# Reordering a two-layer encoder on one core: gates and neighbourhood attention first, retention after them, branch a's product ahead of branch b's block

## The chip, the core and the metric

The kernel runs on one core of a Trainium2 chip. A core has five engines that work side by side, each through its own instruction stream: TensorE (PE: matmuls), VectorE (DVE), ScalarE (ACT), GpSimd (POOL) and SyncE (SP, which here only starts DMA transfers). They share an on-chip memory of 128 partitions (SBUF) and an accumulator memory that TensorE writes (PSUM). The metric is the device time of one execution in microseconds; the median over runs is compared.

## What is computed

A bidirectional encoder of two layers over 512 tokens of width 1024. Cut to what matters:

```python
for i in range(2):
    q_na,k_na,v_na, q_r,k_r,v_r,g_r, gate_a,gate_b = split(x @ w_in[i])
    ya = neighbourhood_attention(q_na, k_na, v_na, rpb[i])        # 8 heads of 64, softmax
    yb = silu(g_r) * groupnorm(retention(q_r, k_r, v_r))          # 4 heads, both directions
    merged = sigmoid(gate_a)*(ya @ w_a[i]) + sigmoid(gate_b)*(yb @ w_b[i])
    x = layer_norm(alpha*x + merged @ w_out[i])                   # token sublayer
    ffn = (gelu(a) * b) @ w_down[i]      # a, b: halves of conv3(x @ w_up[i])
    x = layer_norm(alpha*x + ffn + sigmoid(x @ w_pg[i]) * (p[i] @ w_pp[i]))
```

## The kernel before

Every product is made in about fp32 precision from two halves: a number is split into hi (rounded) and lo (the rest), and each product is three matmuls, hi·hi, lo·hi and hi·lo (`mm3`, L395). A weight chunk is 128x1024 (512 KB). It arrives by DMA as raw, ScalarE makes hi, and VectorE makes lo = raw - hi (`split`, L164). For the chunks in SENT it goes another way: ScalarE makes hi and -hi, and a DMA on POOL's queue that adds while it writes makes lo from the copy of the weights in HBM (L355 to L357).

The four 1024-wide parts of the input projection that are largest (v, g of the retention branch, and the two gates) and branch b's projection are each a block of seven half-size products in place of eight, with sums of weights and sums of activations as operands. The seven are called a, c, t1, d, t2, t3, t4. Blocks 0 and 1 are v and g, blocks 2 and 3 the gates; "3t1" is product t1 of block 3. The weights of t1 to t4 are sums of chunks. `add` (L298) makes such a sum in one of two ways: by a DMA on POOL's queue that adds the second chunk from HBM (L305), or, for the products named in ON_CHIP, by a tensor_tensor of POOL on a chunk that is in SBUF already (rawa or rawt + rawd, L302). The activation sums s are made by VectorE from the transposed x (xf).

A layer's token sublayer has these steps. `vg` walks the table VG: blocks in an order written out by hand, with a few head projections between. Then come the "fillers" in the order of FILL: q and k heads of retention with their rotary step, q and k of neighbourhood attention (nq, nk), and its v (vn). After each filler a slot ends, and the tables RET_AT and NA_AT say in which slot each step of a retention head or of a neighbourhood head is issued. The last seven fillers are branch b's block (`bb`, L1085), whose `emit` multiplies each finished quarter into M, the gate of branch b. In one of its slots `plain_x` loads the residual xn; in layer 1 it also multiplies by the norm's scale and adds its shift, on POOL (L1080, L1081). After the fillers branch a's product follows, and `merge` (L1203) multiplies it with gate a into sa and adds M (L1205, L1206). `turn` (L1208) transposes the merged tile and splits it into mt; `proj_ln` makes the output projection and the layer norm. In a neighbourhood head the exponentials S are scaled by the reciprocal of their sums, rc, by one POOL instruction over 128x1024 (L1035), before TensorE transposes them.

Two things set the order of instructions. From the start, and in the MLP, each engine's instructions are kept in the order of the code; these show line 96 in the profile whatever their own line. From the end of `vg` to the end of the token sublayer a scheduler orders them by their dependencies and shows their own lines. In both, each engine takes its own instructions strictly in turn. Weights are fetched and split ahead of use in the order of one list, `Stream.seq`, with three raw buffers (rp), three pairs of hi and lo buffers (wp), and a pool of thirty 4 KB units (up) for all else.

Of the kernel before, what the change touches and what calls it, by code (L numbers as in the profile page):

```python
# [32 lines left out]
SENT = ((24, 36),)  # L33
# [4 lines left out]
FILL = (('nq0', 'q1', 'nk0', 'k2', 'k1', 'vn', 'q2', 'q3', 'k3', 'nq1', 'nk1', 'nq2', 'nq3', 'nk3', 'nk2'),  # L38
 ('k1', 'q1', 'nk0', 'nk2', 'nq0', 'nq1', 'q2', 'q3', 'k2', 'k3', 'vn', 'nk1', 'nq2', 'nk3', 'nq3'))
BB = ("a", "c", "t1", "d", "t2", "t3", "t4")  # L40
RET_AT = ((5, 6, 13, 14), (3, 5, 11, 11))
NA_AT = ((6, 11, 14, 16, 18, 19, 19, 19), (10, 13, 16, 16, 16, 19, 19, 19))
ORD = ('vector', 'scalar', 'tensor', 'gpsimd', 'sync')
RESIDENT = {(l, c) for l in range(DEPTH) for c in range(68, 72)}
# [3 lines left out]
VG = (('p0', 'p1', '2a', '3a', '3c', '2c', '2t1', '2t2', '3t1', '2d', '3t2', '2t3', '3d', '1a', '3t3', '3t4', '2t4', '0a', '0c', '1c', '0t1', '0d', 'q0',  # L48
  '0t2', '1t1', '0t3', '0t4', 'k0', '1d', '1t2', '1t3', '1t4'),
 ('2a', '2c', '3a', '3c', '3t1', '2t1', '3t2', '2d', '3d', '2t2', '0a', '2t3', '3t3', '0c', '2t4', '1a', 'q0', '0t1', '3t4', '0d', '0t2', '1c', '1t1',  # L50
  '1d', '0t3', '0t4', '1t2', 'k0', '1t3', '1t4'))

XN_AT = 5
M_AT = 4
TABLES_AT = (12, 15)
REST_AT = (1, 3, 5, 8, 10, 12)
PEND_AT = (2, 3)
# [12 lines left out]
VG_HELD = (('0c', '0t1', '1t1', '1t2', '1t4', '2c', '2d', '2t2', '2t3', '3a', '3d', '3t2', '3t3', '3t4'),  # L70
 ('0t1', '0t2', '0t3', '0t4', '1t2', '1t4', '2a', '2c', '2d', '2t1', '2t2', '2t4', '3c', '3t1', '3t2', '3t3'))
ON_CHIP = ('t3', 't2 t3', 't2 t3', 't2 t3')
BB_HELD = ('a', 't1', 't2')
BB_EARLY = 'c'
# [38 lines left out]
def trunk(tc, wpack, x_nat, x_tr, head, p_tr, rpb, decay, ln_par, ln_col, conv, cos_t, sin_t, dist, xi_d, zd, ident_d, out):  # L113
# [4 lines left out]
    with ExitStack() as es:  # L118
# [49 lines left out]
        class Item:  # L168
# [7 lines left out]
            def __init__(self, kind, src, width, pool=None, plus=None, own=None):  # L176
# [4 lines left out]
                self.sent = kind == "w" and any(a <= src[1] < b for a, b in SENT)  # L181
# [40 lines left out]
        def vg_items(l):  # L222

            by = {}
            for b, c0 in enumerate((0, 12, 52, 36)):
                pos = {(q, j): (l, c0 + 2 * i + j, 0, 1024) for i, q in enumerate("acbd") for j in range(2)}
                for it in block_items(pos, {k[1:]: up for k in VG_HELD[l] if k[0] == str(b)}, VG_EARLY, ON_CHIP[b]):
                    it.block = b
                    by.setdefault(f"{b}{it.kind}", []).append(it)
            return [it for k in VG[l] for it in (by[k] if k in by else plain_items(l, k))]  # L230

        def bb_items(l):
# [3 lines left out]
            for it in block_items(pos, {k: up for k in BB_HELD}, BB_EARLY):  # L236
                by.setdefault(it.kind, []).append(it)
# [409 lines left out]
        for l in range(DEPTH):  # L647
# [574 lines left out]
            for t in range(4):  # L1222
                turn(1, t)
# [492 lines left out]
```

## Time and profile before

| | |
|---|---|
| median of 3 runs | 1759.23 us (1758.42 to 1760.92) |
| profiled execution | 1758.02 us, of it span 1756.3 us |
| TensorE busy | 1683.0 us, 96% of the span |
| VectorE busy | 1316.5 us, 75% |
| ScalarE busy | 945.4 us, 54% |
| POOL busy | 294.7 us, 17% |
| mean granted clock of TensorE | 0.982 |
| moved by DMA | 277.35 MB |

Busy time of an engine is the time in which it runs instructions; a wait is idle time before an instruction, shown with the instruction that released it. A group row reads: line, engine, operation, output<-inputs, shapes, count | busy us, mean ns of one | idle time before and what ended it. "PE u L96 <- ACT s L96: 9.8, 1, 9.8" says that TensorE waited 9.8 us in one wait, before a matmul into u, for ScalarE's s. PEclk is the clock granted to TensorE, in tenths in the page's slices (9 is 90% or more) and as a fraction in the stretch table. The token sublayers lie at about 0 to 440 us and 880 to 1320 us, the MLPs behind each.

### The profile page before, as it was taken

The numbers are of one execution on the slowest core, as the hardware profiler recorded it, in microseconds if no ns is written. First come the engines' busy times: TensorE is split into PE (matmuls) and PEld (weight loads), VectorE is DVE, ScalarE is ACT, GpSimd is POOL, SyncE is SP. The second block draws the span as 40 slices with busy tenths as digits, with TensorE's granted clock in tenths as the row PEclk, the third lists the DMA queues.
The fourth block names the chain that finished last, engine by engine and source line by source line (L and its number), as shares of the span: only waits on it lengthen the run. The fifth ranks groups of instructions, "written<-read, shape, count | busy, mean of one in ns | idle before, by whom it ended". The sixth has DMA issues, their size and how long they took to land.

```text
span 1756.3 us, 21209 instructions
## 1 busy us (share of the span) xinstructions
PE 1683.0 (96%) x7815; PEld 1395.4 (79%) x7815; DVE 1316.5 (75%) x1908; ACT 945.4 (54%) x1434; POOL 294.7 (17%) x238
## 2 busy tenths in 40 slices
PE   9699999999999999999988999998889999999997
PEld 7587888877888888888876778887668888888886
DVE  5867568898687867667877766867986878676678
ACT  6555576773266545345555655568622665443452
POOL 1504011320110100000142220122421101000003
PEclk9899999999999999999999999999989999999999
DMA  8686455764754535527766745367538546356375
GB/s 284 186 250 171 108 138 127 173 176 152 219 144 133 131 113 164 143 85 204 199 219 175 200 119 132 85 156 187 161 117 255 144 129 136 107 160 141 96 203 96
DMA packets 81896, 277.35 MB, mean 158 GB/s; under 512 B 9473, under 2 KB 9985, under 8 KB 81793
## 3 DMA queue, kind: packets, MB, share of 16 engines
q1 hardware_dynamic: 60768, 201.55, 33.3%
q0 software_dynamic: 21024, 74.46, 24.8%
q8 instruction: 61, 1.00, 0.2%
q14 instruction: 43, 0.34, 0.1%
HBM read 257.10 MB, written 17.83 MB: 157 GB/s over the span
## 4 chain that ended last, share of the span: by engine, by line
PE 79%; DVE 11%; ACT 4%; DMA 3%; issue 2%; SPq 0%; POOL 0%; DVEq 0%; ACTq 0%; POOLq 0%
PE gt L96 28%; PE u L96 15%; PE v L96 7%; PE w L96 4%; PE gn L398 3%; PE gn L399 3%; PE gn L397 3%; PE gt L399 2%; PE gt L397 2%; PE gt L398 2%; DVE lo L166 2%; DVE lo L96 2%; PE x L96 2%; DVE s L96 1%; ACT hi L96 1%
## 5 line engine op out<-in xcount | busy, mean ns | idle before, releaser
L96 PE MATMUL gt<-x1t,hi 128*128 128x512 f32 x1408 | 433.4, 389 | 0.0
L96 PEld LDWEIGHTS gt<-x1t,hi 128*128 128x128 f32 x1408 | 264.3, 188 | 54.7
L96 PE MATMUL gt<-x1t,lo 128*128 128x512 f32 x704 | 274.1, 389 | 0.1
L96 DVE TENSOR_TENSOR lo<-raw,hi 128x1024 fp32r<-128x1024 f32 (+1 forms) x146 | 174.8, 1206 | 48.5 <-ACT hi L96 48.2
L96 DVE TENSOR_TENSOR lo<-rawa,hi 128x1024 fp32r<-128x1024 f32 x122 | 148.4, 1228 | 72.3 <-ACT hi L96 71.9
L96 DVE SCALAR_TENSOR_TENSOR ca<-gt,cw,ca 128x511 f32<-128x511 f32 x176 | 131.8, 749 | 79.1 <-ACT ca L96 76.0
L96 ACT CAST hi<-raw 128x1024 fp32r<-128x1024 f32 (+1 forms) x149 | 153.0, 1037 | 37.8 <-PE u L96 13.5
L96 PEld LDWEIGHTS gt<-x1t,lo 128*128 128x128 f32 x704 | 132.1, 188 | 28.5 <-DVE lo L96 1.0
L96 ACT CAST hi<-rawa 128x1024 fp32r<-128x1024 f32 x122 | 122.9, 1021 | 52.1 <-DMA rawa<-in_wpack 17.5
L96 ACT ACTIVATE ca<-gt,cw 128x512 f32<-128x512 f32 x88 | 68.6, 779 | 131.4 <-PE gt L96 131.4
L96 POOL DMA_DIRECT2D rawa<-in_wpack x80 | 70.0, 900 | 390.8 <-DVE lo L96 336.6
L96 PE MATMUL u<-hi,s 128*128 128x512 f32 x320 | 105.0, 401 | 11.0 <-ACT s L96 9.8
L96 PE MATMUL v<-hi,s 128*128 128x512 f32 x320 | 106.3, 404 | 9.5 <-ACT hi L96 7.7
L399 PE MATMUL gt<-xt,lo 128*128 128x512 f32 x224 | 87.5, 391 | 1.5 <-DMA lo<-in_wpack 0.8
L397 PE MATMUL gt<-xt,hi 128*128 128x512 f32 x224 | 87.9, 393 | 0.0
L398 PE MATMUL gt<-xt,hi 128*128 128x512 f32 x224 | 87.3, 390 | 0.0
L96 PE MATMUL u<-hi,xt 128*128 128x512 f32 x256 | 81.1, 390 | 3.1 <-DVE p L96 3.1
L96 PEld LDWEIGHTS v<-hi,s 128*128 128x128 f32 x320 | 63.0, 197 | 24.8 <-ACT hi L96 9.0
L96 PEld LDWEIGHTS u<-hi,s 128*128 128x128 f32 x320 | 62.2, 195 | 25.1 <-ACT s L96 10.2
L165 ACT CAST hi<-raw 128x1024 fp32r<-128x1024 f32 x41 | 43.1, 1051 | 57.4 <-PE gn L399 26.0
L96 PE MATMUL v<-lo,s 128*128 128x512 f32 x160 | 65.3, 408 | 6.4 <-DVE lo L96 6.4
L166 DVE TENSOR_TENSOR lo<-raw,hi 128x1024 fp32r<-128x1024 f32 x41 | 50.7, 1237 | 26.6 <-ACT hi L165 26.3
(366 smaller groups left out, 3932.3 us busy)
## 6 DMA issues: line engine op xcount, KB each, us to landing
raw<-in_wpack SPq DMA_DIRECT2D x207, 512.0 KB, 4.1
rawa<-in_wpack POOLq DMA_DIRECT2D x90, 512.0 KB, 5.9
rawa<-in_wpack SPq DMA_DIRECT2D x34, 512.0 KB, 6.4
rawt<-in_wpack SPq DMA_DIRECT2D x34, 512.0 KB, 7.1
lo<-in_wpack POOLq DMA_DIRECT2D x24, 512.0 KB, 5.9
rawt<-in_wpack POOLq DMA_DIRECT2D x18, 512.0 KB, 6.6
rawd<-in_wpack SPq DMA_DIRECT2D x16, 512.0 KB, 9.6
r_scr<-pp SPq DMA_DIRECT2D x8, 512.0 KB, 12.1
```

The lines of the kernel that those rows point to most:

```text
L96: r = f(*a, **k)
L165: nc.scalar.copy(hi, src)
L166: nc.vector.tensor_sub(lo, src, _f(hi))
L397: nc.tensor.matmul(ps, lh, rh, start=start, stop=False, skip_group_check=more)
L398: nc.tensor.matmul(ps, lh, rl, start=False, stop=False, skip_group_check=more)
L399: nc.tensor.matmul(ps, ll, rh, start=False, stop=stop, skip_group_check=more)
```

## The change

The token sublayer is put in another order. VG is now short: it starts with the gate blocks 3 and 2 and a few projections of neighbourhood attention. All else moves to FILL: the rest of the gate blocks, vn and the other na projections, then blocks 0 and 1 (v and g) with the q and k heads, then "ba", branch a's product, and at the end branch b's block. Neighbourhood heads stand early in the slots and retention heads late. `fillers` can therefore emit block products, and only the short VG is kept in the order of the code; the rest is ordered by the scheduler.

With it come: the softmax scaling in four 128x256 pieces, on ScalarE for the heads in RC_ACT (6 and 3 of 8), on VectorE for the others; layer 1's xn operations on VectorE; ON_CHIP empty but for t2 of block 2 in layer 0, so that the other sums of weights are made by accumulating DMA; SENT by names of items, 7 chunks in place of 24; `ba`, which multiplies branch a's product by its gate into sa before branch b's block; the sum with M inside that block's `emit` (L1146, L1147 of the new kernel); turns inside the block, one product late (TURN_LAG); the first half of the output projection made token by token, with its four chunks resident; and new slots for smaller steps.

In counts of instructions: matmuls and transposes 7,828 as before, VectorE 1,910 to 1,963, ScalarE 1,372 to 1,402, of which table loads 30 to 41, POOL 243 to 202, transfers started by SP 424 as before. POOL's tensor_tensor sums of weights fall from 28 to 2, its scalings from 16 to 0, its xn operations from 8 to 0, while its transfers rise by 9, and lo<-hi on ScalarE falls from 24 to 7.

```diff
-FILL = (('nq0', 'q1', 'nk0', 'k2', 'k1', 'vn', 'q2', 'q3', 'k3', ...
+FILL = (('2c', '3t2', '3d', 'nk1', 'vn', '3t3', '3t4', '2t1', 'nk2', '2t2', '2d', '2t3', '0a', 'nq2', ...
-RET_AT = ((5, 6, 13, 14), (3, 5, 11, 11))
+RET_AT = ((33, 32, 38, 37), (31, 38, 36, 39))
-SENT = ((24, 36),)
+SENT = (('k3', 'q2'), ('k2', 'k3', 'nk2', 'nq3', 'q1'))
-VG = (('p0', 'p1', '2a', '3a', '3c', '2c', '2t1', '2t2', '3t1', ...
+VG = (('p0', 'p1', '3a', 'nq0', 'nk3', 'nq3', '3c', '3t1', 'nk0', '2a', 'nq1'), ('3a', '2a', '2c', '3c', '3t1', ...
-ON_CHIP = ('t3', 't2 t3', 't2 t3', 't2 t3')
+ON_CHIP = (('', '', 't2', ''), ('', '', '', ''))
+RC_ACT = ((0, 2, 3, 5, 6, 7), (3, 4, 6))
...
-                s4 = S.rearrange("p (g n) -> p g n", g=4)
-                nc.gpsimd.tensor_tensor(s4, s4, _ap(rc, 0, [[1, 4], [0, 256]]), ALU.mult)
+                for g in range(4):
+                    if h in RC_ACT[l]:
+                        nc.scalar.activation(S[:, g * 256:(g + 1) * 256], S[:, g * 256:(g + 1) * 256], AF.Copy, scale=rc[:, g:g + 1])
+                    else:
+                        nc.vector.tensor_scalar_mul(S[:, g * 256:(g + 1) * 256], S[:, g * 256:(g + 1) * 256], rc[:, g:g + 1])
...
                     if l:
-                        nc.gpsimd.tensor_tensor(z, z, g, ALU.mult)
-                        nc.gpsimd.tensor_tensor(z, z, b, ALU.add)
+                        nc.vector.tensor_mul(z, z, g)
+                        nc.vector.tensor_add(z, z, b)
...
+            def ba():
+                for t in range(4):
+                    sa.append(unit_f("sa"))
+                    nc.sync.dma_start(sa[t], gscr[0][t * P:(t + 1) * P, :])
+                for hb in range(2):
+                    pss = []
+                    for t in gemm_n_tok(lambda k, s, t: yat[k][:, s, t * P:(t + 1) * P], 2, pss, 0):
+                        c = slice(hb * 512, (hb + 1) * 512)
+                        nc.vector.tensor_mul(sa[t][:, c], pss[t], sa[t][:, c])
+                        if t % 2:
+                            yield
...
                     nc.vector.scalar_tensor_tensor(m, src, sign, m, op0=ALU.mult, op1=ALU.mult)
+                    nc.vector.tensor_add(sa[t][:, c], sa[t][:, c], m)
+                    turns.append((hb, t))
...
+                    due = len(turns)
                     step(kind)
+                    for _ in range(due if TURN_LAG else len(turns)):
+                        turn(*turns.pop(0))
                     yield
+                for z in turns:
+                    turn(*z)
...
-            def merge(hb, t, ps):
-                c = slice(hb * 512, (hb + 1) * 512)
-                nc.vector.tensor_mul(sa[t][:, c], ps, sa[t][:, c])
-                nc.vector.tensor_add(sa[t][:, c], sa[t][:, c], M[t][:, c])
```

What this does to the instruction streams is shown at three places. The first is POOL in layer 0's first blocks. Before, with rawa and rawt the chunks that become a sum, and rawd the chunk that is added:

```order
L96 DMA rawa_158<-in_wpack 128x1024
L96 TENSOR_TENSOR rawa_117<-rawa_117,rawd_358 128x1024
L96 TENSOR_TENSOR rawa_121<-rawa_121,rawd_401 128x1024
L96 DMA rawa_117<-in_wpack 128x1024
L96 DMA rawa_121<-in_wpack 128x1024
L96 TENSOR_TENSOR rawt_84_458<-rawt_84_458,rawd_358 128x1024
L96 TENSOR_TENSOR rawa_123<-rawa_123,rawd_477 128x1024
L96 TENSOR_TENSOR rawt_88_480<-rawt_88_480,rawd_401 128x1024
L96 TENSOR_TENSOR rawa_158<-rawa_158,rawd_519 128x1024
```

and now:

```order
L98 DMA rawa_117<-in_wpack 128x1024
L98 DMA rawa_121<-in_wpack 128x1024
L98 DMA rawa_411<-in_wpack 128x1024
L98 DMA rawa_463<-in_wpack 128x1024
L98 DMA rawt_115_652<-in_wpack 128x1024
L98 DMA rawa_117<-in_wpack 128x1024
L98 DMA rawt_121_679<-in_wpack 128x1024
L310 DMA rawa_121<-in_wpack 128x1024
L307 TENSOR_TENSOR rawa_411<-rawa_411,rawd_1069 128x1024
L307 TENSOR_TENSOR rawa_463<-rawa_463,rawd_1088 128x1024
```

The tensor_tensor sums between the transfers are gone but for two, and transfers that add from in_wpack stand in their place.

The second is ScalarE in layer 0's start, around the first block product. Before (hi: a weight half; p: the copy of a product; s and xt: halves of activations):

```order
L96 CAST hi_264<-raw_208 128x1024
L96 COPY p_47_282<-u_244 128x512
L96 COPY p_48_283<-u_245 128x512
L96 CAST hi_296<-raw_210 128x1024
L96 CAST hi_312<-raw_250 128x1024
L96 COPY p_56_328<-u_294 128x512
L96 COPY p_57_329<-u_295 128x512
L96 CAST hi_338<-raw_268 128x1024
L96 CAST hi_354<-rawa_117 128x1024
L96 ACT_TABLE_LOAD
L96 ACTIVATE p_56_328<-p_56_328 128x512
L96 ACTIVATE p_57_329<-p_57_329 128x512
```

and now, where gate block 3 is first, and the next matmuls are those of nq0 on all of xt:

```order
L98 CAST hi_245<-raw_123 128x1024
L98 CAST hi_263<-raw_158 128x1024
L98 COPY p_44_281<-u_243 128x512
L98 COPY p_45_282<-u_244 128x512
L98 CAST xt_106<-xf_125 128x2x256
L98 CAST xt_106<-xf_127 128x2x256
L98 CAST xt_106<-xf_125 128x2x256
L98 CAST xt_106<-xf_127 128x2x256
L98 ACTIVATE dl_299<-dl_299 128x16
L98 CAST hi_320<-raw_204 128x1024
```

The casts of the second half of x (xf_125, xf_127) now stand directly behind the copies of the first product, and ahead of all further weights.

The third is VectorE at layer 1's last turns, with M branch b's gated product, sa the merged tile, mt its transposed halves. Before, where xn stands on POOL (rows not shown):

```order
L1109 SCALAR_TENSOR_TENSOR M_10571<-u_10226,M_10571 128x512
L1109 SCALAR_TENSOR_TENSOR M_10573<-u_10227,M_10573 128x512
L166 TENSOR_TENSOR lo_10845<-raw_10665,hi_10844 128x1024
L1205 TENSOR_TENSOR sa_10776<-gn_10784,sa_10776 128x512
L1206 TENSOR_TENSOR sa_10776<-sa_10776,M_10222 128x512
L1205 TENSOR_TENSOR sa_10778<-gn_10799,sa_10778 128x512
L1206 TENSOR_TENSOR sa_10778<-sa_10778,M_10224 128x512
L1205 TENSOR_TENSOR sa_10780<-gn_10814,sa_10780 128x512
L1206 TENSOR_TENSOR sa_10780<-sa_10780,M_10571 128x512
```

and now:

```order
L1146 SCALAR_TENSOR_TENSOR M_10879<-u_10575,M_10879 128x512
L1146 SCALAR_TENSOR_TENSOR M_10881<-u_10576,M_10881 128x512
L1147 TENSOR_TENSOR sa_10243<-sa_10243,M_10879 128x512
L1147 TENSOR_TENSOR sa_10245<-sa_10245,M_10881 128x512
L1094 TENSOR_TENSOR xn_10939<-xn_10939,lng_10935 128x1024
L1095 TENSOR_TENSOR xn_10939<-xn_10939,lnb_10936 128x1024
L1094 TENSOR_TENSOR xn_10943<-xn_10943,lng_10935 128x1024
L1094 TENSOR_TENSOR xn_10947<-xn_10947,lng_10935 128x1024
L1095 TENSOR_TENSOR xn_10943<-xn_10943,lnb_10936 128x1024
L1095 TENSOR_TENSOR xn_10947<-xn_10947,lnb_10936 128x1024
L1094 TENSOR_TENSOR xn_10951<-xn_10951,lng_10935 128x1024
L168 TENSOR_TENSOR mt_10995<-tr_10989,mt_10994 128x4x128
```

Branch a's product (gn) no longer stands between the additions to sa; the eight xn operations came from POOL, and the halves mt of the last turns stand behind them.

More of the change, by code (lines that the diff above doesn't have):

```diff
@@ L485, in proj_ln @@
             deep = 4 + follow
-            drain(gemm_n(lh, nchunk, [], post=lambda t, ps: half(t, 0, ps), ahead=lambda c: max(2, deep - 2 * (nchunk + n1 - 1 - c))))
+            pss = []
+            for t in gemm_n_tok(lh, nchunk, pss, 0):
+                half(t, 0, pss[t])
             pss = []
```

108 lines of the change are left out of this document (57 added, 51 removed), and 3 rows, old and new, of the table FILL.

## The prediction

> **What bounds the kernel now.** I read the page's engine shares first, then the clock and POOL slices.
>
> ```profile
> PE 1683.0 (96%) x7815; PEld 1395.4 (79%) x7815; DVE 1316.5 (75%) x1908; ACT 945.4 (54%) x1434; POOL 294.7 (17%) x238
> POOL 1504011320110100000142220122421101000003
> PEclk9899999999999999999999999999989999999999
> ```
>
> TensorE is the bound, and the change leaves its 7,828 matmuls as they are. So only time in which TensorE waits, or runs at a lower granted clock, can move. The stretch table says where that is (columns: stretch, length, busy time of PE, PEld, DVE, ACT, POOL, then granted clock, DMA share, GB/s).
>
> ```profile
> 44.00:110.00 66.00, 50.72 (x200) 40.22 (x201) 51.12 (x64) 39.40 (x52) 26.30 (x14) 0.87 0.69 189
> 110.00:176.00 66.00, 62.54 (x275) 51.02 (x274) 45.80 (x42) 37.16 (x49) 22.37 (x12) 1.00 0.74 215
> 360.00:400.00 40.00, 37.80 (x185) 30.97 (x186) 38.63 (x75) 27.45 (x59) 8.38 (x6) 0.96 0.63 165
> 400.00:440.00 40.00, 37.41 (x186) 30.81 (x185) 32.19 (x46) 15.44 (x24) 0.00 (x0) 1.00 0.47 150
> 440.00:880.00 440.00, 439.95 (x1965) 364.45 (x1964) 331.75 (x447) 218.82 (x299) 40.25 (x43) 1.00 0.56 153
> 880.00:920.00 40.00, 35.25 (x155) 28.35 (x154) 30.54 (x29) 23.29 (x36) 15.76 (x8) 0.96 0.67 223
> 920.00:960.00 40.00, 34.61 (x138) 27.36 (x137) 30.93 (x24) 20.81 (x28) 13.66 (x10) 0.91 0.72 173
> 960.00:1040.00 80.00, 75.00 (x321) 60.78 (x320) 53.88 (x51) 44.66 (x57) 22.20 (x13) 0.98 0.61 177
> 1220.00:1260.00 40.00, 38.84 (x208) 33.13 (x208) 37.74 (x75) 30.10 (x64) 8.28 (x6) 0.97 0.63 172
> 1260.00:1290.00 30.00, 17.91 (x65) 13.79 (x64) 29.88 (x25) 8.64 (x14) 22.69 (x8) 0.79 0.21 79
> ```
>
> From 440 to 880 (layer 0's MLP) 1965 matmuls fill the time at full clock: 440 / 1965 = 0.224 us each. With that as the yardstick, a stretch's length minus 0.224 times its matmuls is what it loses, waits and low clock together: 66 - 44.8 = 21.2 us in 44–110, 4.4 in 110–176, 5.3 in 880–920, 9.1 in 920–960, 8.1 in 960–1040, 15.4 in 1260–1290. These six make 63.5 us, and they are the stretches in which POOL is busy. The waits of TensorE name VectorE and ScalarE as the late ones:
>
> ```profile
> PE u L96 <- ACT s L96: 9.8, 1, 9.8
> PE u L397 <- DVE p L708: 8.5, 1, 8.5
> PE v L96 <- DVE lo L96: 6.4, 5, 3.2
> PE tr L1211 <- DVE sa L1206: 3.4, 2, 1.7
> ```
>
> Why VectorE is late shows in two timelines laid side by side (start, length, instruction): first VectorE, then POOL, around 63–76 us, and below them VectorE in the last stretch.
>
> ```profile
> 63.70 3.41 DVE L96 TENSOR_TENSOR lo<-rawd,hi 128x1024 fp32r<-128x1024 f32 x1
> 67.03 5.63 DVE L96 TENSOR_TENSOR s<-xf,xf 128x512 f32<-128x512 f32 x2
> 75.43 1.22 DVE L96 TENSOR_TENSOR lo<-rawa,hi 128x1024 fp32r<-128x1024 f32 x1
> ```
>
> ```profile
> 62.85 3.18 POOL L96 TENSOR_TENSOR rawa<-rawa,rawd 128x1024 f32<-128x1024 f32 x1 [0.16 <-DMA rawd<-in_wpack]
> 65.98 3.37 POOL L96 TENSOR_TENSOR rawt<-rawt,rawd 128x1024 f32<-128x1024 f32 x1
> 69.31 2.79 POOL L96 TENSOR_TENSOR rawa<-rawa,rawd 128x1024 f32<-128x1024 f32 x1
> ```
>
> ```profile
> 1277.04 4.43 DVE L1109 SCALAR_TENSOR_TENSOR M<-p,M 128x512 f32<-128x512 f32 x2
> ```
>
> Beside a POOL tensor operation a lo subtraction takes 3.41 us and an s addition 2.8 us; after POOL falls idle at 72.1 the same subtraction takes 1.22. The last stretch's M products, beside the xn operations on POOL, take 2.2 us each. So a POOL elementwise operation on a large SBUF tile holds up VectorE, and through it the weight halves and sums that TensorE waits for. POOL's own groups:
>
> ```profile
> L96 POOL TENSOR_TENSOR rawt<-rawt,rawd 128x1024 f32<-128x1024 f32 x16 | 43.5, 2754 | 31.4 <-DMA rawt<-in_wpack 31.4
> L96 POOL TENSOR_TENSOR rawa<-rawa,rawd 128x1024 f32<-128x1024 f32 x12 | 34.7, 2894 | 43.7 <-DMA rawd<-in_wpack 31.0 <-DVE lo L96 7.1 <-PE v L96 5.7
> L1035 POOL TENSOR_TENSOR S<-S,rc 128x1024 f32<-128x1024 f32 x16 | 31.0, 1935 | 49.5 <-DVE rc L1033 47.5 <-PE w L399 2.0
> L1080 POOL TENSOR_TENSOR xn<-xn,lng 128x1024 f32<-128x1024 f32 x4 | 11.4, 2862 | 15.2 <-PE v L399 15.2
> L1081 POOL TENSOR_TENSOR xn<-xn,lnb 128x1024 f32<-128x1024 f32 x4 | 11.4, 2842 | 0.3
> ```
>
> **The change, part by part.** *POOL's tensor work goes.* Of the 28 on-chip weight additions two remain (t2 of block 2, layer 0); the 16 softmax scalings and 8 xn operations leave POOL. The POOL sums 43.5 + 34.7 + 31.0 + 11.4 + 11.4 = 132 us shrink to about 6. All of the 63.5 us could go; at the other end, where the late operand was late for its own load, only part goes. One such load is on the chain that ended last:
>
> ```profile
> 27.70 17.56 DMA rawd<-in_wpack
> ```
>
> That rawd transfer, to be added on POOL, opens the 9.8 us wait, and it goes with the change too. I take -63.5 and charge 3 us for waits in these stretches that have another cause (0 to 10).
>
> *The weights added by DMA instead.* 26 adds become accumulating transfers on POOL's queue, and 17 chunks that were split by ScalarE and an accumulate are split by VectorE. Per layer the token part lasts 440 us, so nine more 512 KB transfers in all are small beside DMA shares of 0.47 to 0.74 there. Their cover is the look-ahead of the weight stream. Nothing charged; if a transfer is late, that is the 3 us above.
>
> *The softmax scaling.* Sixteen heads times four 128x256 pieces: 36 go to ScalarE, 28 to VectorE. Prices by the nearest rows:
>
> ```profile
> L940 DVE TENSOR_SCALAR yb<-yb,rstd 128x256 f32<-128x256 f32 x32 | 10.0, 350 | 5.4 <-POOL rstd L447 5.4
> L901 ACT ACTIVATE kz<-kz,zeta 128x128 fp32r<-128x128 f32 x32 | 11.6, 366 | 4.9 <-DVE kz L902 4.8
> L1030 ACT ACTIVATE S<-S,nmx 128x256 f32<-128x256 f32 x64 | 31.9, 501 | 10.7 <-DVE nmx L1025 10.7
> L96 ACT ACT_TABLE_LOAD x28 | 35.9, 1283 | 2.0 <-DVE ca L96 0.8 <-PEq L1709 0.7
> L356 ACT ACTIVATE lo<-hi 128x1024 fp32r<-128x1024 f32 x21 | 22.3, 1062 | 0.4
> L96 DVE TENSOR_TENSOR lo<-raw,hi 128x1024 fp32r<-128x1024 f32 (+1 forms) x146 | 174.8, 1206 | 48.5 <-ACT hi L96 48.2
> ```
>
> VectorE: 28 x 0.350 = 9.8 us, the same form. ScalarE: between 366 (half the elements) and 501 (same size, exponential), so 0.45 taken, 36 x 0.45 = 16 us; 11 more table loads are 14 us; 17 fewer lo<-hi give back 17 x 1.06 = 18. So ScalarE gains 12 us, and VectorE 9.8 + 17 x 1.21 (splits) + 8 x 1.21 (xn) = 40 us, while it is freed of the slowing. A head's scaling takes 4 x 0.35 = 1.4 or 4 x 0.45 = 1.8 us in place of 1.94 on POOL, so its chain to the transposes is no longer. But gates and neighbourhood heads now share one stretch, with weights cast there too. Behind other matmuls most is hidden: I charge 4 us (0 if all is covered; 26 if half of the 52 us shows).
>
> *The first block.* Layer 0 now runs 3a, then nq0 directly. nq0 needs the second half of x, whose casts stand on ScalarE's queue behind the two copies of 3a's result:
>
> ```profile
> 18.29 1.04 ACT xt L96 x2
> L96 ACT COPY p<-u 128x512 f32<-128x512 f32 x20 | 11.8, 595 | 13.5 <-PE u L96 13.4
> ```
>
> Two copies (1.2), two casts (1.04) and one subtraction on VectorE (0.7): TensorE waits 2.9 us, or 3.9 if all four casts are needed. I take 3. On ScalarE everything behind those copies moves with them, weight casts first.
>
> *Branch b's block alone.* Before, heads and other fillers stood between its products; now they are done by then, branch a's product as well, and each M product is followed by an addition to sa. Between the block's start and its last addition VectorE has 57 rows per layer: 13 halves of weights (13 x 1.21 = 15.7) and 44 of 128x512 (44 x 0.685 = 30.1, by the row of the same operation below), 46 us.
>
> ```profile
> L1206 DVE TENSOR_TENSOR sa<-sa,M 128x512 f32<-128x512 f32 x16 | 11.0, 689 | 0.3
> ```
>
> TensorE has 7 products of 24 matmuls, 168 x 0.224 = 37.6 us, and the turns of finished quarters, about 4 us. VectorE is therefore late by 46 - 42 = 4 to 46 - 37.6 = 8.4 us: 6 per layer. Behind the last product come two M products and two additions before the last turns, 4 x 0.69 = 2.8 us, of which the earlier turns hide a part: 2 per layer. In layer 1 the eight xn operations (9.7 us) stand on VectorE between the last additions and the lo halves of the last turns, which the third token of the output projection needs; two tokens of it come first, 36 matmuls or 8 us, so 2.5 us shows. Together 18.5. What the present kernel loses at these places goes: 40 - 37.80 = 2.2, 40 - 37.41 = 2.6 and 40 - 38.84 = 1.2 us of idle TensorE, 6.0 in all (the tr waits are in it). Net +12.5, between +6 and +23.
>
> *The clock.* The clock fell to 0.96 in 360–400, though the longest wait there is short:
>
> ```profile
> PE ns L1021 <- DVE nmx L1025: 1.1, 1, 1.1
> ```
>
> With new waits of 2 to 6 us in each block I expect one more low window per layer; 0.04 of 40 us is 1.6 each, 3 us in all (0 to 7). The Trainium skill's page "TensorE: Matmul & The Clock Gate", section "Part 1: The HAM clock gate", has the clock fall after an idle window of about 3.4 us. By that rule waits of 1 us each would cost no clock, and this term would be 0 and the time 1718; the trace here disagrees, since the clock fell with no wait above 1.1 us.
>
> **Sum** against the profiled execution: -63.5 + 3 + 4 + 3 + 12.5 + 3 = -38.0. That execution took 1758.0 us (span 1756.3) where the median is 1759.2, so 1720 by it, 1721 by the median.
>
> **The rivals.**
> - *The block is wholly VectorE-bound.* Nothing of the 8.4 us is covered, the whole chain of 2.8 shows, xn shows whole (9.7) and two low windows fall in each block (3.2 per layer): 2 x 14.4 + 9.7 - 6 = 32.5 in place of 15.5, so 1738. For it: VectorE is at 37.74 of 40 us in 1220–1260 already. Against: instructions overlap a little, and weights can be split ahead.
> - *Late accumulates.* A weight made by a transfer onto another has to wait for two landings in a row. If one in each of the eight v, g and gate blocks is late by 3 us, 24 us come back: 1745. Against: accumulates run from 440 to 880 too, at a DMA share of 0.56, and TensorE loses nothing there.
> - *Slower: POOL was not what slowed VectorE*, but the transfers into the same tiles. Then slowed operations stay slow, the 40 us of new VectorE work come on top in stretches where TensorE already waits for it, and only the 9.8 us wait for rawd and its half-clock tail (5) go: 1759 + 40 - 15 = 1784 if all shows. It is slower from 15 us shown. Against: 1.22 us at 75.43, in a stretch with a DMA share of 0.69, and only POOL had stopped.
> - *The moved order hides its own losses elsewhere*, so that gains and new waits cancel: needs 38 us more of waits than charged, which no row shows.
>
> **Chances.** Forecast as summed (1700 to 1733): 0.60. Block bound: 0.15. Late accumulates: 0.11. Slower: 0.10. Cancelled: 0.04, of which 0.03 within 0.2%, about what a measurement of this kernel can tell from no change. So faster 0.87, same 0.03, slower 0.10. The best case, all of 63.5 for only 3 + 6 of charges, is 1705, or 1696 with none; the range reaches from there to 1752, beyond the late accumulates.
>
> **What would show it.** Right: no large POOL tensor operation left but the two weight sums and the two at the very end; the s additions and the M products at 0.68 us; PEclk 1.0 in the first fortieths and no dip at layer 1's end; waits of TensorE for DVE in the seven products of each layer. Wrong: VectorE operations above 2 us with POOL idle, waits for rawa or rawt transfers, or ScalarE full in the stretch of the heads with TensorE waiting on S.

## The result, and the profile after

| | before | after |
|---|---|---|
| median | 1759.35 us (1758.42 to 1760.92, 4 runs) | 1695.34 us (1695.12 to 1695.81, 4 runs) |
| ratio | | 0.9636, 95% interval 0.9619 to 0.9652 |
| profiled execution, span | 1758.02, 1756.3 us | 1695.12, 1693.4 us |
| mean granted clock | 0.982 | 0.997 |

The kernel became 64 us faster. The forecast was 1721 with a range from 1696 to 1752: the time lies 0.7 us under the range. The page after, answering to the three lines of it that the prediction began with:

```profile
PE 1665.3 (98%) x7815; PEld 1383.2 (82%) x7815; DVE 1283.6 (76%) x1961; ACT 956.2 (56%) x1464; POOL 177.2 (10%) x197
POOL 0101101110200100100111111010102010000003
PEclk9999999999999999999999999999999999999999
```

The stretch table, after. The token sublayer of layer 0 now ends some 10 us earlier and that of layer 1 begins near 860, so the second and third rows answer to 880–920 and 920–960 of before, and the last to the end of layer 1's block.

```profile
44.00:110.00 66.00, 64.20 (x277) 51.16 (x276) 43.88 (x59) 47.70 (x71) 6.93 (x8) 1.00 0.75 210
860.00:900.00 40.00, 40.00 (x186) 33.33 (x186) 30.31 (x39) 30.45 (x48) 5.08 (x6) 1.00 0.91 274
900.00:940.00 40.00, 40.00 (x177) 32.59 (x176) 23.25 (x27) 25.89 (x39) 1.92 (x3) 1.00 0.64 160
1240.00:1265.00 25.00, 22.66 (x100) 18.14 (x99) 22.20 (x26) 6.26 (x8) 0.00 (x0) 0.93 0.71 253
```

TensorE runs 277 matmuls in 44–110 where it ran 200. The same view in three pieces, token sublayers and MLP, first before and then after:

```profile
0.00:440.00 440.00, 413.44 (x2007) 342.69 (x2008) 328.76 (x528) 269.56 (x442) 94.72 (x74) 0.98 0.65 177
880.00:1320.00 440.00, 404.11 (x1956) 336.36 (x1955) 330.68 (x492) 254.05 (x423) 113.93 (x75) 0.96 0.57 156
```

```profile
0.00:430.00 430.00, 420.20 (x2061) 348.18 (x2062) 323.55 (x555) 280.23 (x465) 47.14 (x56) 1.00 0.68 190
860.00:1300.00 440.00, 432.87 (x2148) 362.92 (x2148) 338.69 (x566) 270.14 (x455) 49.53 (x56) 1.00 0.69 188
```

Idle TensorE in the two sublayers fell from 26.6 + 35.9 = 62.5 us to 9.8 + 7.1 = 16.9; that is 45.6 of the 62.9 us by which the span shrank. The other 17 are busy time: the same matmuls took 1683.0 us before and take 1665.3 now, at a mean granted clock of 0.997 in place of 0.982. The waits of TensorE that are left:

```profile
PE u L403 <- DVE lo L168: 2.2, 1, 2.2
PE tr L1102 <- DVE sa L1147: 2.2, 2, 1.7
PE gn L404 <- DVE mt L168: 1.8, 1, 1.8
PE gt L98 <- ACT xt L98: 1.2, 1, 1.2
PE u L402 <- ACT mt L167: 1.2, 1, 1.2
```

And VectorE is no longer slowed: the s additions, 1815 ns in the mean before, and the M products of p, 1297 ns before, are at their bare durations:

```profile
L98 DVE TENSOR_TENSOR s<-xf,xf 128x512 f32<-128x512 f32 x8 | 5.2, 687 | 0.1
L1146 DVE SCALAR_TENSOR_TENSOR M<-p,M 128x512 f32<-128x512 f32 x8 | 5.2, 686 | 0.0
```

So far this reads as the prediction's mechanism at full size. The experiments say otherwise.

### The profile page after: what moved, and what is told of

It is laid out like the page before. It is cut to its first block, busy times and chain, and to the rows that moved or that the text cites. A ratio compares the mean times of both kernels' runs of the same rounds, so it can differ in the third digit from the quotient of the medians.

```text
span 1693.4 us, 21234 instructions
## 1 busy us (share of the span) xinstructions
PE 1665.3 (98%) x7815; PEld 1383.2 (82%) x7815; DVE 1283.6 (76%) x1961; ACT 956.2 (56%) x1464; POOL 177.2 (10%) x197
## 4 chain that ended last, share of the span: by engine, by line
PE 83%; DVE 9%; ACT 3%; issue 2%; DMA 1%; POOL 0%; SPq 0%; DVEq 0%; POOLq 0%; ACTq 0%
PE gt L98 29%; PE u L98 9%; PE v L98 4%; PE w L98 3%; PE gn L404 3%; PE gn L402 3%; PE gn L403 3%; PE u L403 3%; PE u L402 3%; PE u L404 3%; PE gt L402 2%; PE gt L403 2%; PE gt L404 2%; DVE lo L168 2%; PE x L98 2%
## 5 line engine op out<-in xcount | busy, mean ns | idle before, releaser
L167 ACT CAST hi<-raw 128x1024 fp32r<-128x1024 f32 x78 | 81.4, 1051 | 71.3 <-DMA raw<-in_wpack 32.8
L168 DVE TENSOR_TENSOR lo<-raw,hi 128x1024 fp32r<-128x1024 f32 x78 | 95.1, 1228 | 33.2 <-ACT hi L167 32.8
L168 DVE TENSOR_TENSOR lo<-rawa,hi 128x1024 fp32r<-128x1024 f32 x69 | 84.0, 1223 | 27.6 <-ACT hi L167 27.3
L98 DVE TENSOR_TENSOR lo<-rawa,hi 128x1024 fp32r<-128x1024 f32 (+1 forms) x73 | 84.2, 1163 | 24.8 <-ACT hi L98 24.5
L167 ACT CAST hi<-rawa 128x1024 fp32r<-128x1024 f32 x69 | 71.9, 1051 | 54.7 <-DMA rawa<-in_wpack 23.4
L98 ACT CAST hi<-rawa 128x1024 fp32r<-128x1024 f32 (+1 forms) x73 | 72.3, 1003 | 35.5 <-PE v L98 14.4
L98 POOL DMA_DIRECT2D rawa<-in_wpack x59 | 51.5, 879 | 312.7 <-DVE lo L98 275.4
L402 PE MATMUL gt<-xt,hi 128*128 128x512 f32 x192 | 75.3, 392 | 1.1 <-DVE t L854 0.7
L403 PE MATMUL gt<-xt,hi 128*128 128x512 f32 x192 | 74.9, 390 | 0.0
L310 POOL DMA_DIRECT2D rawa<-in_wpack x47 | 42.1, 895 | 281.0 <-DVE lo L168 266.3
L98 PE MATMUL v<-hi,sa 128*128 128x512 f32 x176 | 56.1, 389 | 0.0
L404 PE MATMUL gn<-hi,mt 128*128 128x512 f32 x128 | 49.9, 395 | 1.8 <-DVE mt L168 1.8
```

Of the source, the lines that this page charges most:

```text
L98: r = f(*a, **k)
L167: nc.scalar.copy(hi, src)
L168: nc.vector.tensor_sub(lo, src, _f(hi))
L310: nc.gpsimd.dma_start(it.raw[:, :w], wpack[l, c][:, o:o + w], accum_op=ALU.add)
L402: nc.tensor.matmul(ps, lh, rh, start=start, stop=False, skip_group_check=more)
L403: nc.tensor.matmul(ps, lh, rl, start=False, stop=False, skip_group_check=more)
```

## The experiments

The ratios below are against the kernel before, which ran beside each of these kernels (medians of 1759.2 to 1759.9 us). In the sections on the new order "slower" and "faster" are against the 1695.3 us above, unless "before" is named; the changed kernel was not run again beside them.

### POOL freed in the old order

Four kernels keep the order of the kernel before and take POOL's work away, part by part and together. The weight sums:

```diff
-ON_CHIP = ('t3', 't2 t3', 't2 t3', 't2 t3')
+ON_CHIP = ('', '', '', '')
```

> The kernel before with one table changed: ON_CHIP empty, so all 28 weight sums are made by accumulating DMA and none by POOL. Order, softmax scaling and xn stay. Theory 1 (POOL's large tensor operations slow VectorE, and TensorE waits for that): the loss of the stretches 44-176 and 880-1040 (21.2 + 4.4 + 5.3 + 9.1 + 8.1 = 48 us by the yardstick) goes but for some 8 us: 1719 +- 10 us, s additions at 0.68 us and lo subtractions at 1.22 us there, although more transfers run. Theory 2 (the new order makes the gain, POOL's part is small): 1750 or above. Theory 3 (the sums were late for the load of rawd, not for POOL's hold on VectorE): only the 9.8 us wait and its clock go, 1744.

Measured 1746.1 us (ratio 0.9926, 0.9911 to 0.9940). The figure lies next to theory 3's, but for another reason: the 9.8 us wait, which theory 3 has go, is still 7.1 us. VectorE was freed, as theory 1 has it (a pair of s additions 1.29 us, a lo subtraction 1.22):

```profile
61.63 1.29 DVE L96 TENSOR_TENSOR s<-xf,xf 128x512 f32<-128x512 f32 x2
...
64.55 1.22 DVE L96 TENSOR_TENSOR lo<-raw,hi 128x1024 fp32r<-128x1024 f32 x1 [0.26 <-ACT hi L96]
73.91 1.22 DVE L96 TENSOR_TENSOR lo<-rawa,hi 128x1024 fp32r<-128x1024 f32 x1 [8.13 <-ACT hi L96]
```

But the last row has 8.13 us of idle VectorE ahead of it. In the stretch table of this run TensorE does no more in 44–110 than before, and the DMA engines are full (0.99, where the kernel before had 0.69); the waits of ScalarE from 40 to 176 us name the transfers:

```profile
44.00:110.00 66.00, 51.57 (x197) 40.06 (x197) 39.40 (x64) 38.46 (x51) 10.47 (x12) 0.87 0.99 255
```

```profile
ACT hi L96 <- DMA rawa<-in_wpack: 28.3, 6, 8.3
```

So in layer 0's start a blocked VectorE was exchanged for weights that come late. Sums by transfer load the DMA engines more than their bytes say: from 40 to 110 us POOL's queue, which carries them, took 58.2% of the engines' time for 7.52 MB, SP's queue 41.1% for 10.36 MB.

The 13 us that this run gained lie in layer 1's gate blocks; layer 0 ends no earlier than before (the same instruction of its last norm starts at 880.33 us there and at 881.92 here). The same stretch of 160 us, before and in this run:

```profile
880.00:1040.00 160.00, 144.86 (x610) 116.49 (x609) 115.35 (x103) 88.77 (x121) 51.61 (x30) 0.96 0.65 188
880.00:1040.00 160.00, 154.63 (x675) 125.54 (x674) 99.97 (x115) 97.92 (x135) 26.78 (x31) 0.99 0.91 242
```

65 matmuls more, at 0.224 us each, are some 15 us. There theory 1 holds, although the DMA share is 0.91 there. Why they keep up there and not in layer 0's start was not tested. The xn operations and the softmax scaling, each alone:

```diff
-                        nc.gpsimd.tensor_tensor(z, z, g, ALU.mult)
-                        nc.gpsimd.tensor_tensor(z, z, b, ALU.add)
+                        nc.vector.tensor_mul(z, z, g)
+                        nc.vector.tensor_add(z, z, b)
```

> The kernel before with layer 1's eight xn operations on VectorE in place of POOL, nothing else. Theory 1: the 15.4 us lost in 1260-1290 go, 8 x 1.21 = 9.7 us of VectorE work come back there, of which 3 to 6 show: 1747 +- 4 us. Theory 2 or 3: VectorE is busy 29.88 of 30 us in that stretch already, so 9.7 us more of work show as they are: 1765 or above.

```diff
-                nc.gpsimd.tensor_tensor(s4, s4, _ap(rc, 0, [[1, 4], [0, 256]]), ALU.mult)
+                for g in range(4):
+                    if h in ((0, 2, 3, 5, 6, 7), (3, 4, 6))[l]:
+                        nc.scalar.activation(S[:, g * 256:(g + 1) * 256], S[:, g * 256:(g + 1) * 256], AF.Copy, scale=rc[:, g:g + 1])
+                    else:
+                        nc.vector.tensor_scalar_mul(S[:, g * 256:(g + 1) * 256], S[:, g * 256:(g + 1) * 256], rc[:, g:g + 1])
```

> The kernel before with the softmax scaling in four pieces on ScalarE and VectorE (as the changed kernel shares them out), nothing else. Theory 1: the 16 scalings on POOL (31.0 us) slow VectorE too, but lie in stretches in which TensorE loses little; a gain of 0 to 6 us, 1756 +- 4. Theory 2: 16 us more on ScalarE and 10 us more on VectorE, in the old order, cost 0 to 10 us: 1759 to 1769.

xn on VectorE: 1753.7 us (0.9965, 0.9954 to 0.9977), between the two expectations. Of the 15.4 us at that place about 6 were gained; the products still waited 6.1 us for p. Scaling: 1760.5 us (1.0006, 0.9997 to 1.0016), no difference. The three together:

> The three edits together: the kernel before, in its old order, with no large tensor operation on POOL in the token sublayers. Theory 1: nearly all of the gain of 64 us, 1700 to 1715 us. Theory 2: less than 25 us of gain, 1735 or above; the rest is the order's. In between, the share of each is read off.

Measured 1744.8 us (0.9917, 0.9902 to 0.9932): 15 us of gain, not 45 to 60. Theory 1 as I held it, that POOL alone makes the gain, falls. Its stretches:

```profile
44.00:110.00 66.00, 50.47 (x193) 39.71 (x192) 38.86 (x64) 37.48 (x50) 10.47 (x12) 0.87 0.99 250
...
1150.00:1210.00 60.00, 51.26 (x315) 45.25 (x313) 39.77 (x110) 40.95 (x88) 9.79 (x12) 0.97 0.73 174
1210.00:1245.00 35.00, 32.94 (x167) 28.03 (x168) 31.99 (x73) 26.59 (x59) 2.62 (x3) 0.91 0.51 121
1245.00:1275.00 30.00, 24.02 (x104) 19.24 (x104) 28.90 (x39) 12.89 (x21) 0.00 (x0) 0.89 0.39 150
```

Layer 0's start loses as before, on transfers. At the end of layer 1's token sublayer TensorE idles 8.7 + 2.1 + 6.0 = 16.8 us in 1150–1275, with POOL doing nothing large.

### Neither POOL nor the transfers, in the old order

```diff
-                    nc.gpsimd.tensor_tensor(it.raw, it.raw, it.other.raw, ALU.add)
                     return
```

> The kernel before with its 28 on-chip weight sums left out altogether: the chunks rawa and rawt are used unsummed (so that part of the result is another), no POOL operation and no extra transfer stands in their place. With the sums made by DMA (the run above of that name) VectorE's s additions fell to 0.65 us and the lo subtractions to 1.22, but TensorE still lost as much in 44-110, now waiting for ScalarE's hi, which waited for rawa, at a DMA share of 0.99. Theory A (in the old order that stretch is bound by transfers once POOL is off): without the extra transfers the loss of 44-176 and 880-1040 goes from 48 us to 10 or so, 1719 +- 8 us. Theory B (the old order's own chains, products behind s and casts, hold TensorE there whatever brings the weights): at least 15 us stay in 44-176, 1735 or above.

Measured 1722.3 us (0.9792, 0.9778 to 0.9807): theory A, for the most part. TensorE runs 260 matmuls in 44–110:

```profile
44.00:110.00 66.00, 60.81 (x260) 49.82 (x261) 44.07 (x67) 44.67 (x59) 6.03 (x7) 0.97 0.86 246
```

Against 1746.1 with the sums as transfers, those transfers cost the old order 24 us. With scaling and xn off POOL as well (this edit and the two of the section above):

> The kernel before, in its old order, with the 28 weight sums left out (neither POOL nor a transfer makes them, so that part of the result is another) and scaling and xn off POOL. What is left is what the old order loses by itself when neither POOL nor the extra transfers hold it up. If the order costs nothing of its own: near 1695. If it does: 1722 (sums left out, scaling and xn still on POOL) less at most 8 for xn, 1712 to 1722, with the loss in the last 120 us of layer 1's token sublayer.

Measured 1722.0 us (0.9788, 0.9773 to 0.9803). So 27 us above the changed kernel are the old order's own: neither POOL nor the sums have a part in them. They lie where expected, in layer 1's end (TensorE idles 8.3 + 6.2 us in 1180–1255, at a clock of 0.83 and 0.90), and some at the start (5.2 us idle in 44–110, most of it behind s):

```profile
PE u L396 <- DVE p L707: 5.9, 2, 5.4
PE u L396 <- DVE pt L166: 5.7, 1, 5.7
PE u L96 <- ACT s L96: 4.2, 1, 4.2
```

### POOL's work put back in the new order

The reverse edits, on the changed kernel. The weight sums (ON_CHIP as the kernel before had it):

```diff
-ON_CHIP = (('', '', 't2', ''), ('', '', '', ''))
+ON_CHIP = (('t3', 't2 t3', 't2 t3', 't2 t3'), ('t3', 't2 t3', 't2 t3', 't2 t3'))
```

> The changed kernel with ON_CHIP as the kernel before had it (28 weight sums on POOL in place of 2), its order kept. Theory A (order and POOL each would do it alone, the new order gives every weight time to come): VectorE is slowed where the sums fall, but TensorE loses at most 8 us: 1696 to 1703. Theory B (the hold on VectorE costs wherever it falls): half or more of the 48 us comes back: 1719 or above.

Measured 1726.0 us (0.9802, 0.9783 to 0.9820; runs from 1721.4 to 1731.0): 31 us slower, theory B. So the new order does not make the hold harmless. TensorE waits 4.9 + 3.5 + 3.2 us for lo halves in it (its profile is of the slowest of these runs):

```profile
PE u L403 <- DVE lo L168: 4.9, 3, 2.3
PE w L403 <- DVE lo L98: 3.5, 1, 3.5
PE w L403 <- DVE lo L168: 3.2, 2, 1.8
```

Ahead of the lo half that the 3.5 us wait names, at 78.7 us, stands an operation of VectorE on a 128x16 tile, of 0.17 us elsewhere, that took 2.33 beside a sum on POOL:

```profile
74.06 2.53 POOL L98 TENSOR_TENSOR rawt<-rawt,rawd 128x1024 f32<-128x1024 f32 x1 [9.24 <-DMA rawt<-in_wpack]
74.30 2.33 DVE L98 TENSOR_SCALAR dl<-dl 128x16 f32<-128x16 f32 x1
```

A fourth wait for lo, 2.5 us at 38.5 us, is not the hold: POOL has no sum there, VectorE waited 7.8 us for the load of dl, and a kernel below with only two sums on POOL has the same wait.

The softmax scaling:

```diff
-                for g in range(4):
-                    if h in RC_ACT[l]:
...
+                s4 = S.rearrange("p (g n) -> p g n", g=4)
+                nc.gpsimd.tensor_tensor(s4, s4, _ap(rc, 0, [[1, 4], [0, 256]]), ALU.mult)
```

> The changed kernel with the softmax scaling back on POOL, 16 instructions of 1.9 us. If POOL's hold costs there: 3 to 8 us slower, 1698 to 1703. If ScalarE's 18 us and VectorE's 10 us of scaling cost as much as the hold: within 2 us of 1695. In the old order the same edit the other way changed nothing (1760.5 against 1759.5).

Measured 1703.3 us (0.9684, 0.9668 to 0.9700), 8 us slower. The same edit that changed nothing in the old order is worth 8 us in the new one. xn:

```diff
-                        nc.vector.tensor_mul(z, z, g)
-                        nc.vector.tensor_add(z, z, b)
+                        nc.gpsimd.tensor_tensor(z, z, g, ALU.mult)
+                        nc.gpsimd.tensor_tensor(z, z, b, ALU.add)
```

> The changed kernel with the eight xn operations of layer 1 back on POOL. If the hold on VectorE is what costs at the tail, M, sa and mt take 2 us and more beside them and TensorE loses 5 to 12 us more: 1700 to 1707. If the 9.7 us on VectorE cost as much themselves as the hold, nothing moves: 1693 to 1698.

Measured 1691.1 us (0.9612, 0.9597 to 0.9626; runs 1690.0 to 1691.8 against 1695.1 to 1695.8): 4 us *faster* than the changed kernel, which neither expectation had. POOL's hold is there. In 1200–1300 the lo subtractions take 1823 ns in the mean, and the groups of xn are as long as before:

```profile
L168 DVE TENSOR_TENSOR lo<-raw,hi 128x1024 fp32r<-128x1024 f32 x13 | 23.4, 1823 | 0.1
```

```profile
L1094 POOL TENSOR_TENSOR xn<-xn,lng 128x1024 f32<-128x1024 f32 x4 | 11.6, 2896 | 24.1 <-DMA xn<-x_scr 24.1
```

But these lo halves are wanted later, while on VectorE xn stands ahead of the mt halves that are wanted at once. With xn on POOL the last mt halves come first and the slowed subtractions behind them:

```profile
1247.30 2.48 DVE L168 TENSOR_TENSOR mt<-tr,mt 128x512 fp32r<-128x512 f32 x4
1249.70 8.81 DVE L168 TENSOR_TENSOR lo<-raw,hi 128x1024 fp32r<-128x1024 f32 x3
```

The wait for mt (1.8 us) is gone, and the clock in 1240–1265 is 1.00. All three edits together:

> The changed kernel with all three parts back on POOL: weight sums, softmax scaling, xn. What is left is the order alone. Theory A (the order gives most): 1715 or below. Theory B (POOL gives most, once the order lets it): 1730 or above. The old order with POOL freed took 1744.8, so the two together show whether the parts add (1759 - 15 - x = 1695 would mean 1710) or need each other.

Measured 1715.2 us (0.9753, 0.9738 to 0.9767), 44 us faster than before with all of POOL's work still in place. The two orders and the two places of that work make a square:

| | on POOL | off POOL | difference |
|---|---|---|---|
| old order | 1759.4 | 1744.8 | -15 |
| new order | 1715.2 | 1695.3 | -20 |
| difference | -44 | -49 | |

The larger part is the order's, if "new order" is taken for all of the change that these three edits leave: the tables of the order, but also the 17 chunks taken out of SENT, branch a's product ahead of branch b's block, the turns inside it and the output projection with resident chunks. The runs below take parts of the tables and the lag of the turns one at a time; the rest was not tried alone. In 44–176, where the old order lost on weights, it has no transfer of SENT. The parts do not add: the sums alone on POOL (1726) were slower than all three (1715). The scheduler orders the rest of the sublayer anew for each kernel, and the runs cannot tell its share from the edit's.

### Which part of the order

Layer 0, the gate products (all but 2t4) in one run and the projections behind them:

```diff
-VG = (('p0', 'p1', '3a', 'nq0', 'nk3', 'nq3', '3c', '3t1', 'nk0', '2a', 'nq1'), ...
+VG = (('p0', 'p1', '3a', 'nq0', '3c', '3t1', '2a', '3t2', '2c', '3d', '3t3'), ...
-FILL = (('2c', '3t2', '3d', 'nk1', 'vn', '3t3', '3t4', '2t1', 'nk2', '2t2', '2d', '2t3', '0a', ...
+FILL = (('3t4', '2t1', '2t2', '2d', '2t3', 'nk0', 'vn', 'nk3', 'nq3', 'nq1', 'nk1', 'nk2', '0a', ...
-NA_AT = ((10, 13, 13, 16, 18, 19, 20, 23), ...
+NA_AT = ((13, 14, 16, 17, 18, 19, 20, 23), ...
```

> The changed kernel, layer 0 alone: the fourteen products of the two gate blocks in one run, with only nq0 among them, and the other projections of neighbourhood attention, vn and the heads behind them; all else as in the changed kernel. So the same work, but the products that need two chunks and sums for 5.4 us of TensorE are no longer mixed with projections that need one chunk for 5.4 us. If the mixing is what the order gives at the start: the DMA share in 44-110 rises to 0.9 and above, ScalarE waits for rawa, and 10 to 25 us come back in 44-176: 1705 to 1720. If it was something else (the gates first, or the short hand-ordered part): within 5 us of 1695.

Measured 1715.4 us (0.9748, 0.9733 to 0.9762): 20 us slower, with layer 1 untouched. The stretch falls back to 229 matmuls, TensorE waits for hi, and ScalarE for a chunk that has not come:

```profile
44.00:110.00 66.00, 58.04 (x229) 44.99 (x228) 35.99 (x45) 38.76 (x53) 12.54 (x11) 0.92 0.81 225
```

```profile
PE u L95 <- ACT hi L95: 4.0, 2, 3.3
```

```profile
ACT hi L95 <- DMA rawt<-in_wpack: 6.9, 2, 6.3
```

The mean DMA share is 0.81, not the 0.9 I expected, but where that chunk is late the transfers are full (1.05 in the next row), and the mean hides it. The chunk is a sum made by two transfers in a row. POOL waited 11.5 us for the first to land before it started the second, for which ScalarE waited until 73.8:

```profile
54.00:74.00 20.00, 15.39 (x63) 11.31 (x62) 8.17 (x15) 6.98 (x10) 0.87 (x1) 0.99 1.05 300
```

```profile
65.39 0.87 POOL L95 DMA_DIRECT2D rawt<-in_wpack  x1 [11.53 <-DMA rawt<-in_wpack]
```

Layer 1, the last neighbourhood heads later:

```diff
-NA_AT = (..., (6, 9, 9, 10, 11, 11, 17, 20))
+NA_AT = (..., (6, 9, 9, 10, 14, 16, 28, 33))
```

> The changed kernel, layer 1 alone: neighbourhood heads 4 to 7 start in slots 14, 16, 28, 33 in place of 11, 11, 17, 20, so that the last ones stand among the retention heads, just ahead of branch a's product and branch b's block. If crowding of heads at the layer's end is what the order took away there (with POOL freed but the order kept TensorE still lost over 20 us in 1150-1275): 5 to 15 us slower, 1700 to 1710, with waits for pt, S or yat. If not: within 2 us of 1695.

Measured 1738.8 us (0.9880, 0.9848 to 0.9913; runs 1731 to 1746): 43 us slower, far more than expected, and not where expected. The loss lies in the v and g products out of which the heads were taken, and among the retention heads (where the changed kernel ran 283 and 339 matmuls):

```profile
1060.00:1120.00 60.00, 49.61 (x212) 40.24 (x211) 35.55 (x49) 29.31 (x36) 4.40 (x5) 0.92 0.59 156
1120.00:1180.00 60.00, 52.35 (x247) 41.96 (x247) 35.40 (x75) 32.05 (x59) 3.28 (x4) 0.88 0.21 53
```

```profile
PE gt L402 <- DVE nmx L1036: 8.3, 1, 8.3
PE s L402 <- ACT qk L167: 5.7, 3, 5.2
```

The 8.3 us wait is put down to nmx, but ScalarE shows what held the queue just then: a weight cast that waited 4.5 us for its chunk, ahead of what TensorE needed.

```profile
1111.03 1.04 ACT L167 CAST hi<-rawt 128x1024 fp32r<-128x1024 f32 x1 [4.52 <-DMA rawt<-in_wpack]
```

Here the transfers are not full (0.59 and 0.21). SP starts the loads strictly in turn, and from 1060 to 1200 us it stood 89.0 us in 13 waits for a lo subtraction, that is for a raw buffer to come free. The 5.2 us wait for qk, at 1194, is no wait for a weight: VectorE is busy from 1183 to 1194 with the work of retention heads, with few gaps.

One reading fits both runs: a block product asks for two chunks, sums, casts and splits in 5.4 us of TensorE, a projection for one chunk, a head for none. Mixed, they give each chunk time to arrive; in a run, the products go at the pace of the weights. That the run of gate products costs 20 us in layer 0, on a chunk that comes late, is shown; in layer 1 the reading covers a part of the loss at most. One rival is open. The gates' results are stored through SP's queue too, and in 30–110 SP waited 21.8 us for ScalarE's p in the run of gate products and 29.5 in the old order with POOL freed, 4.2 in the changed kernel; no run separates loads that queue behind such a store from the weights' own pace. For layer 1's end in the old order nothing was tried.

### Two parts of the block's term

```diff
-                    if l:
-                        nc.vector.tensor_mul(z, z, g)
-                        nc.vector.tensor_add(z, z, b)
```

> The changed kernel without layer 1's eight xn operations at all (the residual is then not scaled and shifted, so the result is another). It prices the term that I put at 2.5 us: if the 2.0 us wait for mt is all they cost, 1693; if they also delay layer 1's norm and the clock dip at 1240-1265, as the run with xn on POOL (4 us faster) suggests, 1688 to 1691.

Measured 1689.8 us (0.9611, 0.9595 to 0.9627): xn on VectorE costs 5.5 us where I had 2.5. Without it the wait for mt (1.8), the later one for xn (1.5) and the clock dip to 0.93 in 1240–1265 (0.07 x 25 = 1.75) are all gone; they make 5.1 of the 5.5.

```diff
-TURN_LAG = 1
+TURN_LAG = 0
```

> The changed kernel with TURN_LAG 0: each finished quarter is turned right behind the product that finishes it, not one product later. TensorE then meets a turn whose sa is not added yet: two M products and two additions, 2.8 us, at three places more per layer, where nothing covers them. If the lag is what keeps my block term small: 4 to 12 us slower, 1699 to 1707. If not: within 1.5 us of 1695.

Measured 1704.1 us (0.9688, 0.9674 to 0.9703): 9 us slower. TensorE waits for sa five times:

```profile
PE tr L1102 <- DVE sa L1147: 7.8, 5, 3.0
```

The one-product lag is what keeps the turns out of the way.

The last edit tried for a faster kernel, xn on POOL and the last two sums by DMA:

```diff
-ON_CHIP = (('', '', 't2', ''), ('', '', '', ''))
+ON_CHIP = (('', '', '', ''), ('', '', '', ''))
-                        nc.vector.tensor_mul(z, z, g)
-                        nc.vector.tensor_add(z, z, b)
+                        nc.gpsimd.tensor_tensor(z, z, g, ALU.mult)
+                        nc.gpsimd.tensor_tensor(z, z, b, ALU.add)
```

> The changed kernel with the eight xn operations on POOL and the last two weight sums by DMA. xn on POOL alone took 1691.1 in place of 1695.3. The two sums hold VectorE for 4.8 us in layer 0, where TensorE loses almost nothing: 0 to 1.5 us more, 1690 to 1691.

Measured 1693.2 us (0.9623, 0.9609 to 0.9638): no better than xn on POOL alone, which at 1691.1 is the fastest complete version here, faster than both kernels.

## Why the prediction was wrong, by its own steps

- *Where the loss is: right.* The six stretches nearly emptied. In 44–110 TensorE ran 277 matmuls, in 860–940 it was never idle, and the clock is 0.997. At layer 1's end a dip to 0.93 is left, where the signs of being right had none.
- *"POOL's tensor work goes ... I take -63.5": the failed step.* That POOL slows VectorE is right, and gone (1815 to 687 ns). That this was what the 63.5 us were worth is wrong: POOL freed in the old order gave 15, in the new one 20. I had seen that TensorE waits where VectorE is slow, and did not ask what would be late next. In layer 0's start, in the old order, it is the weights: the DMA share in 44–110 went from 0.69 to 0.99 and the loss stayed. The kernel before showed it already. Its longest wait, 9.8 us up to 53.65, fell where VectorE was itself idle for 7.9 us, behind a chunk that was loaded late and then summed:

```profile
45.42 4.63 POOL L96 TENSOR_TENSOR rawa<-rawa,rawd 128x1024 f32<-128x1024 f32 x2 [19.02 <-DMA rawd<-in_wpack]
48.87 2.28 DVE L96 TENSOR_TENSOR lo<-rawa,hi 128x1024 fp32r<-128x1024 f32 x1 [7.87 <-ACT hi L96]
```

The prediction named that load and had the wait go with the sums; with the sums by transfer, in the old order, 7.1 us of it stayed. In layer 1's gate blocks the step held: some 15 us came back there.
- *"The weights added by DMA ... Nothing charged": right for the changed kernel only.* I named "the look-ahead of the weight stream" as the cover. In layer 0 the cover is the new order, with block products among projections and heads; without it in layer 0 20 us came back (that it is the mixing, and not the stores in SP's queue, is argued). So the part of the change that I priced at nothing, the new order with what belongs to it, carries 44 to 49 of the 64 us. The rival of late accumulates described layer 0's start in the old order with POOL freed; that its 1745 meets the 1744.8 of that run is chance, since it put a loss into each of the eight blocks.
- *The charges of 31.5 us, less a credit of 6.0, so 25.5 net: the terms that put the forecast too high.* The rest of the token sublayers lost 16.5 us of idle TensorE before (62.5 less 46.0 in the six stretches), and everything together loses 16.9 after. So new waits only replaced old ones, and the net is about 0 where I had 25.5. The small credit is a part of it only: with all 16.5 credited and the charges kept, the sum is 1711, and the charges were too large as well. That -63.5 alone comes so close to the measured 64 is luck, since most of the gain is not what it stood for.
- *The block: 18.5 charged.* The waits in the two layers come to 2.2 + 2.2 + 1.8 + 1.2 us in the rows above, and 1.1 for yw and u (0.7 and 0.4), 8.5 in all. Of "4 to 8.4 us per layer" for a late VectorE little is seen. The lag of the turns keeps 9 us of it away; why the products themselves hardly wait was not tested. xn was sized too small, 2.5 for 5.5.
- *The first block: 3 us charged, 1.2 of wait for xt seen* (the wait row above). *Scaling:* the durations were near (0.348 us on VectorE for 0.350, 0.500 on ScalarE for 0.45), but instead of a charge the move is worth 8 us in this order; what POOL's scalings hold up there was not traced. *Clock:* one dip, 1.75 us, for 3.
- *The slower rival,* that transfers and not POOL slow VectorE, is refuted by the first run: 0.65 and 1.22 us at a DMA share of 0.99.

## What to carry to other kernels

A slowed engine beside a waiting one is a lead, not a price: ask what the waiting engine would wait for next, and look whether that resource has room in the same stretch (here the DMA share in layer 0's start, 0.69 before and 0.99 with POOL freed). A full share is a warning and no proof: in layer 1's gate blocks 0.91 cost TensorE little. Weight-hungry products seem to want light work between them; the other order, with what belongs to it, moved this kernel two to three times as far as taking the contention away. When new waits replace old ones, credit the old ones everywhere, not only at the places one has looked at.

## What the runs showed of the hardware

A large elementwise operation on POOL slows VectorE operations whose two inputs lie in SBUF: 128x512 additions from 0.69 to 2.8 us, 128x1024 subtractions from 1.22 to 3.4. The Trainium skill's page "GPSIMD Engine Reference", section "1. Specifications", says that POOL shares SBUF interfaces with VectorE and contends with instructions that have two SBUF inputs; the traces agree. VectorE's single-input scalings, 28 of them in the changed kernel, show no effect on the mean time in which POOL starts a transfer: 895 ns, as in the kernel before.

```profile
L310 POOL DMA_DIRECT2D rawa<-in_wpack x47 | 42.1, 895 | 281.0 <-DVE lo L168 266.3 <-ACT mt L167 8.4 <-DVE pt L168 3.7
```

The clock fell to 0.93 in 1240–1265 of the changed kernel, and the whole fall lies right behind one wait, the 1.84 us for mt that ended at 1258.15. For 8 us ahead of that wait TensorE was never idle:

```profile
1258.00:1260.00 2.00, 1.85 (x5) 1.46 (x6) 2.00 (x4) 0.00 (x0) 0.00 (x0) 0.60 0.00 0
1260.00:1262.00 2.00, 2.00 (x7) 1.58 (x6) 2.00 (x2) 0.00 (x0) 0.00 (x0) 0.55 0.59 158
```

The 2.2 us wait for lo, at 384–386 of the same run, left the clock at 1.00. So the length of the wait alone does not decide it. An idle window of 3.4 us, as the Trainium skill's page "TensorE: Matmul & The Clock Gate" has it in "Part 1: The HAM clock gate", stands before neither this fall nor the one in 360–400 before, where no wait was above 1.1 us.
